# Where the last two of eight activation slots start in SBUF

## The chip, the cores and the metric

The kernel runs on one core of one Trainium2 chip. Times are device microseconds of that core; lower is better. Three runs of the kernel before took 2431.09, 2432.85 and 2435.11 us (median 2432.85).

## The reference, cut to what matters

Two transformer layers are run on 128 context tokens and 128 latent tokens, both with 2048 channels, in float32. Layer 0 mixes with differential attention beside a Conformer convolution; layer 1 mixes with an S5 state-space scan beside grouped-query attention. After each mixer there is an MLP with a squared ReLU. In short:

```
for l in range(2):
    h = rms_norm(x) * g * (1 + scale) + shift        # scale, shift, gate from ada_w[l]
    x = x + gate1 * mixer_l(h)                       # h @ w_in, heads, @ w_out
    h = rms_norm(x) * g2 * (1 + scale2) + shift2
    a = relu(h @ mlp_w1[l])                          # 2048 -> 8192
    x = x + gate2 * ((a * a) @ mlp_w2[l])            # 8192 -> 2048
y = rms_norm(x) * final
```

Every weight matrix is read once, and is multiplied by all 256 tokens.

## The kernel before

**Split products.** Activations lie channel-major: a tile is 128 channels by 256 tokens. Each float32 operand of the large products is split in two halves that TensorE takes as `float32r`: a high half (the value rounded) and a low half (value less high half). ScalarE rounds (`wh` for weights, the first 256 columns of an `hl` tile for activations) and VectorE subtracts (`wl`, and the columns 256 to 511 of `hl`). A 128x128 block of weights then takes three matmuls of 256 columns (`block`, line 517): `wh` by the high half, `wh` by the low half, `wl` by the high half. TensorE loads the 128x128 weights anew ahead of each of the three.

**Parts.** A weight piece is 128 x 1024: eight blocks, one for each of eight activation tiles. `part` (line 524) takes one piece and issues its 24 matmuls; the tiles of an operand are numbered k, and the place of a tile in its part is k % 8. A product with 2048 input channels is two parts, one on the tiles 0 to 7 and one on the tiles 8 to 15. A new piece is loaded by SP's DMA queue, rounded and subtracted while earlier parts run.

**Where the activation tiles lie.** `Arena` (line 75) is one SBUF tile, `hl`, of 12,592 float32 per partition. It holds three groups, each for the eight tiles of one half of an operand (`h0`, `h1`, `mix0`, `mix1`, `yhl`, `hid`), 4,224 elements apart (`GROUP`). Slot j of a group starts at `j * 512` elements, that is every 2,048 bytes; 128 elements of a group stay free behind its eighth slot. The arena starts at byte 42,368 of the partition, 384 past a multiple of 512; a group is 33 times 512 bytes and a half of a slot is 1,024 bytes, so the high and the low half of every slot of every group start at 384 past a multiple of 512. The weights `wh` and `wl` lie 64 past a multiple of 512, at every block.

Two kinds of tile differ. Some MLP tiles lie in the pool `hid` instead of the arena (of each MLP chunk of layer 0, and of layer 1, the tiles 0 to 7, and in one chunk of layer 1 all sixteen); these too start at 384 past a multiple of 512. And at three places the next product starts before its norm is known (`unnormed_tile`, line 816): there the tiles have 2 x 258 columns (`WIDE`), slot j starts at `j * 516` elements, so that the high halves of successive slots start at 384, 400, 416, ... 496 past a multiple of 512, and the low halves 1,032 bytes further on, at 392, 408, ... 504.

**The order of the work.** The program runs twice at build time: once to write down an order of all steps from estimated costs and due times (`charge`, `pick`), and once to issue the instructions in that order. `Arena.tile` (line 104) tells the planner when the columns that a new tile takes come free: the latest use of any tile that owned one of them. Costs do not depend on addresses.

Of the kernel before, what the change touches and what calls it, by code (L numbers as in the profile page):

```python
# [10 lines left out]
F32R = mybir.dt.float32r  # L11
# [37 lines left out]
class Engine:  # L49


    def __init__(self, kern, name, eng):
        self.kern, self.name, self.eng = kern, name, eng
# [11 lines left out]
class Pool:  # L65
# [3 lines left out]
    def tile(self, shape, dtype, name, tag=None, bufs=None):  # L69
        kw = {"tag": tag} if tag else {}  # L70
        if bufs:
            kw["bufs"] = bufs
        t = self.pool.tile(shape, dtype, name=name, **kw)
        self.kern.placed(t, (self.name, tag or name), bufs or self.bufs)
        return t


class Arena:
# [1 line left out]

    SLOT, GROUP, WIDE = 512, 8 * 512 + 128, 516

    def __init__(self, kern, pool):
        self.kern, self.n = kern, 0
        size = 2 * self.GROUP + 8 * self.WIDE
        self.all = pool.tile([128, size + 16], F32R, name="hl")
        self.name = self.all.tensor.name
        self.owner, self.mine = [None] * size, {}  # L90
        self.unused, self.groups = [0, 1, 2], {}
# [11 lines left out]

    def tile(self, part, j, wide=False):
        width = self.WIDE if wide else self.SLOT
        a = self.groups[part] * self.GROUP + j * width
        token = f"hl.{self.n}"
        self.n += 1
        k = self.kern
        k.free_at[token] = max(k.last.get(o, (0, 0))[0] for o in self.owner[a:a + width])  # L110
        self.owner[a:a + width] = [token] * width
        t = self.all[:, a:a + width]
        self.mine[id(t)] = t, token
        return t
# [1875 lines left out]
```

## Time and profile before

| | |
|---|---|
| median of 3 runs | 2432.85 us |
| profiled execution, its own time | 2435.42 us |
| span from first to last instruction | 2433.7 us |
| TensorE busy | 2349.4 us, 97% |
| VectorE, ScalarE, GpSimd busy | 70%, 47%, 7% |
| DMA | 627.64 MB, 258 GB/s |
| mean granted TensorE clock | 0.983 |

Read the row of TensorE first, then how many matmuls stand on `hl` operands, and then how far apart their starts are. The busy time of a matmul in the profile (about 280 ns) is longer than the step from one start to the next (about 118 ns), since matmuls are pipelined; the steps between starts set the time of a stream of matmuls.

### The profile page before, as it was taken

The page shows a single profiled execution, that of the slowest core. Times are in us where ns is not written, and L with a number is a line of the kernel's source. Part 1 is how long each engine was busy: PE and PEld are TensorE (multiplying, and loading weights), DVE is VectorE, ACT ScalarE, POOL GpSimd, SP SyncE. Part 2 cuts the span into 40 slices and gives each one's busy share as a digit, 9 for nine tenths or more (in the row PEclk, how much of TensorE's full clock was granted, in tenths as well). Part 3 has the DMA queues.
Part 4 walks back from the last instruction along what each step waited for, and adds up shares of the span by engine and source line. Part 5 has one row for each costly group of instructions (what it writes and reads, how often), then busy time and mean ns, then how long its engine had stood idle before and what let it go on. Part 6 is the DMA issues. An engine that isn't in the chain of part 4 may idle for free.

```text
span 2433.7 us, 49506 instructions
## 1 busy us (share of the span) xinstructions
PE 2349.4 (97%) x20152; PEld 2147.6 (88%) x20152; DVE 1698.4 (70%) x2957; ACT 1152.6 (47%) x1894; POOL 173.0 (7%) x293
## 2 busy tenths in 40 slices
PE   6999999999999999999999978999999999999997
PEld 1788887888999999999999857699999999999997
DVE  1489985677888889987666434567998855555565
ACT  2364467565434434434455644455744333443443
POOL 0000000000111011101000345000000000000000
PEclk9999999999999999999999988999999999999999
DMA  9979987879678898879877877765587755555552
GB/s 383 332 252 330 317 311 256 294 268 319 202 265 301 295 318 297 317 263 323 285 225 245 292 286 261 268 217 180 196 291 265 271 185 185 187 189 185 186 184 90
DMA packets 179637, 627.64 MB, mean 258 GB/s; under 512 B 21376, under 2 KB 21392, under 8 KB 179152
## 3 DMA queue, kind: packets, MB, share of 16 engines
q1 hardware_dynamic: 169920, 595.67, 70.6%
q0 software_dynamic: 9488, 28.81, 3.8%
q8 instruction: 158, 2.59, 0.4%
q14 instruction: 71, 0.58, 0.1%
HBM read 602.17 MB, written 26.41 MB: 258 GB/s over the span
## 4 chain that ended last, share of the span: by engine, by line
PE 86%; DMA 4%; DVE 3%; POOL 3%; ACT 3%; issue 1%; DVEq 0%; SPq 0%; ACTq 0%; POOLq 0%
PE lin L60 76%; PE ada L60 5%; POOL rt L60 2%; DMA raw<-in_ada_w 1%; DVE wl L60 1%; POOL hs L60 1%; ACT wh L60 1%; DMA raw<-in_ew_in 1%; PE m1T L60 1%; ACT hs L60 1%; PE po L60 1%; DMA raw<-m3d 1%; PE sc L60 0%; PE ps L60 0%; DMA raw<-in_w 0%
## 5 line engine op out<-in xcount | busy, mean ns | idle before, releaser
L60 PE MATMUL lin<-hl,wh 128*128 128x256 f32 (+1 forms) x11200 | 2022.1, 282 | 5.7 <-ACT wh L60 5.5
L60 PEld LDWEIGHTS lin<-hl,wh 128*128 128x128 f32 x11200 | 1718.7, 189 | 97.3 <-issue 61.5
L60 PE MATMUL lin<-hl,wl 128*128 128x256 f32 (+1 forms) x5600 | 1571.1, 281 | 11.1 <-DVE wl L60 11.0
L60 PEld LDWEIGHTS lin<-hl,wl 128*128 128x128 f32 x5600 | 1057.7, 189 | 13.7 <-DVE wl L60 13.6
L60 DVE TENSOR_TENSOR wl<-raw,wh 128x1024 fp32r<-128x1024 f32 (+1 forms) x716 | 858.6, 1207 | 283.4 <-ACT wh L60 276.3
L60 ACT CAST wh<-raw 128x1024 fp32r<-128x1024 f32 (+1 forms) x716 | 737.8, 1034 | 531.0 <-PE lin L60 285.3
L60 PE MATMUL ada<-raw,condp 128*32 128x512 f32 (+1 forms) x1408 | 190.5, 579 | 19.4 <-ACT sq L60 12.9
L60 DVE SCALAR_TENSOR_TENSOR x<-lin,mod,x 128x128 f32<-128x128 f32 x320 | 97.2, 346 | 104.5 <-PE lin L60 104.1
L60 DVE SCALAR_TENSOR_TENSOR va<-raw,condp,va 128x1024 f32<-128x1024 f32 x120 | 148.6, 1280 | 0.0
L60 ACT ACTIVATE ms<-lin 128x256 f32<-128x256 f32 x114 | 43.7, 383 | 159.4 <-PE lin L60 159.4
L60 PEld LDWEIGHTS ada<-raw,condp 128*32 128x32 f32 x1408 | 33.1, 109 | 75.6 <-DMA raw<-in_ada_w 34.8
L60 ACT CAST hl<-mq 128x256 fp32r<-128x256 f32 x128 | 51.9, 406 | 98.4 <-DVE mq L60 98.2
L60 DVE SCALAR_TENSOR_TENSOR cv<-cin,pke,cv 128x256 f32<-128x256 f32 x232 | 96.7, 478 | 0.0
L60 DVE SCALAR_TENSOR_TENSOR mq<-lin,ms 128x256 f32<-128x256 f32 x114 | 48.1, 422 | 64.9 <-ACT ms L60 64.7
L60 ACT ACTIVATE sq<-x 128x256 f32<-128x256 f32 x75 | 30.9, 416 | 116.4 <-DVE x L60 114.3
L60 DVE TENSOR_TENSOR hl<-mq,hl 128x256 fp32r<-128x256 f32 x128 | 53.8, 422 | 27.8 <-ACT hl L60 27.8
L60 POOL TENSOR_TENSOR x<-x,rb 128x512 f32<-128x512 f32 (+1 forms) x2 | 4.2, 2132 | 928.7 <-ACT rb L60 928.7
L60 DVE TENSOR_TENSOR acc<-acc,sq 128x256 f32<-128x256 f32 x75 | 31.8, 424 | 32.3 <-ACT sq L60 30.5
L60 DVE TENSOR_TENSOR hl<-h,hl 128x256 fp32r<-128x256 f32 (+1 forms) x112 | 45.4, 420 | 9.2 <-ACT hl L60 8.9
L60 ACT CAST hl<-h 128x256 fp32r<-128x256 f32 (+1 forms) x112 | 42.8, 402 | 12.5 <-DVE h L60 12.1
L60 POOL DMA_DIRECT2D m3d<-m x32 | 21.5, 677 | 348.3 <-DVE m L60 347.1
L60 DVE TENSOR_TENSOR w<-s5z,bc 128x576 f32<-128x576 f32 x64 | 45.6, 753 | 0.6
(281 smaller groups left out, 1167.5 us busy)
## 6 DMA issues: line engine op xcount, KB each, us to landing
raw<-in_w SPq DMA_DIRECT2D x512, 512.0 KB, 5.1
raw<-in_ada_w SPq DMA_DIRECT2D x352, 512.0 KB, 6.0
raw<-in_ew_in SPq DMA_DIRECT2D x68, 512.0 KB, 6.1
raw<-in_ow_in SPq DMA_DIRECT2D x40, 512.0 KB, 6.6
raw<-in_ada_w SPq DMA_DIRECT2D x64, 256.0 KB, 6.2
raw<-in_ew_out SPq DMA_DIRECT2D x32, 512.0 KB, 5.8
raw<-in_ow_out SPq DMA_DIRECT2D x32, 512.0 KB, 4.7
m3d<-m POOLq DMA_DIRECT2D x32, 256.0 KB, 6.4
```

The costliest lines, as they stand in the source:

```text
L60: return f(out, *a, **kw)
```

## The change

`Arena.tile` adds `SHIFT[j]` elements to the start of a slot with 2 x 256 columns: nothing for j = 0 to 5, 32 elements (128 bytes) for j = 6 and 40 elements (160 bytes) for j = 7. Slot 6 then starts at 0 and slot 7 at 32 past a multiple of 512 bytes, in all three groups, high and low half alike. The wide slots and the tiles of the pool stay where they are. The arena keeps its 12,592 elements (the 16 that were added at the allocation are now counted in `size`), so no other tile moves.

```diff
-    SLOT, GROUP, WIDE = 512, 8 * 512 + 128, 516
+    SLOT, GROUP, WIDE, SHIFT = 512, 8 * 512 + 128, 516, (0, 0, 0, 0, 0, 0, 32, 40)
...
-        size = 2 * self.GROUP + 8 * self.WIDE
-        self.all = pool.tile([128, size + 16], F32R, name="hl")
+        size = 2 * self.GROUP + 8 * self.WIDE + 16
+        self.all = pool.tile([128, size], F32R, name="hl")
...
-        a = self.groups[part] * self.GROUP + j * width
+        a = self.groups[part] * self.GROUP + j * width + (0 if wide else self.SHIFT[j])
```

## Rows read from the trace of the kernel before

**Rows 1.** The page: busy time of each engine, share of the span, instructions.
```profile
PE 2349.4 (97%) x20152; PEld 2147.6 (88%) x20152; DVE 1698.4 (70%) x2957; ACT 1152.6 (47%) x1894; POOL 173.0 (7%) x293
```

**Rows 2.** The page: shares of the chain that ended last, by engine and line.
```profile
PE 86%; DMA 4%; DVE 3%; POOL 3%; ACT 3%; issue 1%; DVEq 0%; SPq 0%; ACTq 0%; POOLq 0%
PE lin L60 76%; PE ada L60 5%; POOL rt L60 2%; DMA raw<-in_ada_w 1%; DVE wl L60 1%; POOL hs L60 1%; ACT wh L60 1%; DMA raw<-in_ew_in 1%; PE m1T L60 1%; ACT hs L60 1%; PE po L60 1%; DMA raw<-m3d 1%; PE sc L60 0%; PE ps L60 0%; DMA raw<-in_w 0%
```

**Rows 3.** Tile hl: operation, count, ns min/median/max, first and last start.
```profile
L60 PE MATMUL lin<-hl,wh x11200: 276/279/775, 66.4 to 2417.1; 128*128 128x256 f32 x186, 128*128 128x258 f32 x11
L60 PE MATMUL lin<-hl,wl x5600: 276/280/582, 67.7 to 2417.2; 128*128 128x256 f32 x183, 128*128 128x258 f32 x11
L60 ACT CAST hl<-h x112: 388/403/412, 58.8 to 1739.7; 128x256 fp32r<-128x256 f32 x64, 128x258 fp32r<-128x258 f32 x48
L60 DVE TENSOR_TENSOR hl<-h,hl x112: 411/419/429, 60.0 to 1741.0; 128x256 fp32r<-128x256 f32 x64, 128x258 fp32r<-128x258 f32 x48
L60 PE MATMUL ps<-hl,wh x64: 276/276/276, 1589.4 to 1608.2; 128*128 128x256 f32 x64
L60 PE MATMUL ps<-hl,wl x32: 276/276/276, 1589.6 to 1608.3; 128*128 128x256 f32 x32
```

**Rows 4.** Groups of TensorE by form: the wide matmuls, count, busy us, mean ns.
```profile
L60 PE MATMUL lin<-hl,wh 128*128 128x258 f32 x608 | 112.2, 286 | 0.0
L60 PE MATMUL lin<-hl,wl 128*128 128x258 f32 x304 | 85.9, 283 | 2.1 <-DVE wl L60 2.1
```

**Rows 5.** Chain in order of time, longest pieces: start us, length us, what.
```profile
463.38 40.35 PE lin L60 x342
...
691.67 17.88 PE lin L60 x156
...
981.56 12.25 PE lin L60 x108
...
1741.43 95.91 PE lin L60 x812
...
1932.04 485.49 PE lin L60 x4122
```

**Rows 6.** TensorE in order of time, 1589 to 1592.2 us: start, length, what.
```profile
1589.40 0.39 PE L60 MATMUL ps<-hl,wh 128*128 128x256 f32 x2
1589.63 0.28 PE L60 MATMUL ps<-hl,wl 128*128 128x256 f32 x1
...
1592.12 0.28 PE L60 MATMUL lin<-hl,wh 128*128 128x256 f32 x1
```

**Rows 7.** TensorE in order of time, 1707.1 to 1713 us, wide tiles.
```profile
1707.27 0.40 PE L60 MATMUL lin<-hl,wh 128*128 128x258 f32 x2
1707.51 0.28 PE L60 MATMUL lin<-hl,wl 128*128 128x258 f32 x1
...
1712.67 0.40 PE L60 MATMUL lin<-hl,wh 128*128 128x258 f32 x2
```

**Rows 8.** TensorE in order of time, 1720.5 to 1724.2 us, wide tiles.
```profile
1721.62 0.41 PE L60 MATMUL lin<-hl,wh 128*128 128x258 f32 x2
...
1723.83 0.41 PE L60 MATMUL lin<-hl,wh 128*128 128x258 f32 x2
```

**Rows 9.** TensorE in order of time, 550 to 552 us: from wide tiles to narrow.
```profile
550.77 0.39 PE L60 MATMUL lin<-hl,wh 128*128 128x256 f32 x2
551.00 0.28 PE L60 MATMUL lin<-hl,wl 128*128 128x256 f32 x1
551.12 0.40 PE L60 MATMUL lin<-hl,wh 128*128 128x256 f32 x2
551.36 0.28 PE L60 MATMUL lin<-hl,wl 128*128 128x256 f32 x1
551.47 0.40 PE L60 MATMUL lin<-hl,wh 128*128 128x256 f32 x2
551.71 0.28 PE L60 MATMUL lin<-hl,wl 128*128 128x256 f32 x1
551.83 0.40 PE L60 MATMUL lin<-hl,wh 128*128 128x256 f32 x2
```

**Rows 10.** Stretches: us, TensorE busy (count), granted clock, DMA share, GB/s.
```profile
1931.00:2415.00 484.00, 484.00 (x4109) 1.00 0.53 179
1572.00:1586.00 14.00, 14.00 (x125) 1.00 0.79 277
```

## The prediction

> **What bounds the kernel now.** I read the page's busy times first: TensorE is busy for 97% of the span and no other engine for over 70% [rows 1]. The chain of waits agrees: 86% of it is TensorE, 76% the matmuls that write `lin` [rows 2]. Next the count of matmuls on `hl` operands: 11,200 + 5,600 + 64 + 32 = 16,896 [rows 3], of which 608 + 304 = 912 are wide [rows 4]. The question is how far apart their starts lie. In the chain, the longest unbroken piece has 4,122 matmuls in 485.49 us [rows 5], 117.78 ns each, at the full granted clock [rows 10]; two others give 95.91 / 812 = 118.1 and 40.35 / 342 = 118.0 ns. I call this the slow rhythm. The same instruction on the same kind of addresses also runs in a quick rhythm: from 1589.40 to 1592.12 us stand 24 matmuls, 2.72 us, 113.33 ns each [rows 6], and the stretch from 1572 us shows 125 in 14 us [rows 10], 112 with the one or two cut at its edges counted whole; the chain pieces at 981.56 and 691.67 us (113.4 and 114.6 ns) are quick too [rows 5]. The clock is 1.00 in both, so it is no matter of the clock. A stream keeps its rhythm until something stops it.
>
> So about 16,896 x 117.78 ns = 1,990 us of the span is this stream, of which the chain counts 76% x 2433.7 = 1,850 us. A nanosecond more or less in each of its matmuls is therefore worth 0.93 of itself at the end.
>
> **What the change touches.** No instruction is added, removed or moved to another engine; the edits of `size` leave the allocation as it was. The pool of the MLP takes 8 of 16 tiles for each of four chunks in two layers and all 16 for one chunk, over 16 outputs each: (8 + 1) x 16 = 144 parts, 3,456 matmuls. The arena's narrow slots therefore have 16,896 - 912 - 3,456 = 12,528 matmuls, 522 parts, and two of eight slots 3,132 of them, six in a part.
>
> Three things could change. First, the writers: ScalarE's round and VectorE's subtraction into `hl` take 403 and 419 ns at the median and spread by only 24 and 18 ns over 112 tiles [rows 3], of which 48 are wide and lie at other addresses. I cost them at nothing; both engines have idle time (47% and 70% busy) [rows 1], and were every fourth of these 112 tiles 24 ns slower, it would be 0.7 us on engines that are hardly on the chain [rows 2]. Second, the planner: a narrow tile 6 now covers columns of the wide tiles 6 and 7 in place of 5 and 6, so a free time can change, but a group is given back only after the last of its readers, and costs don't depend on addresses. I cost it at nothing, give or take 1 us. Third, and this is the term that counts, the steps of TensorE between starts.
>
> **The step at another address.** No row shows a 256-column matmul anywhere but at 384 past a multiple of 512, so 0 and 32 must be bounded. The nearest rows are the wide ones, whose high halves lie at 384 to 496 in steps of 16 and whose low halves lie 8 past those. From 1707.27 to 1712.67 us stand 45 of them, 5.40 us, 120.0 ns each [rows 7]. Two columns more are worth 2 / 2.4 GHz = 0.83 ns (estimate from the two clock levels), which leaves 119.2, or 1.4 ns over the slow rhythm. The dear end is the stretch from 1721.62 to 1723.83, 18 in 2.21 us, 122.8 ns [rows 8], 122.0 without the two columns: 4.2 ns over. The cheap end is the quick rhythm, 4.45 ns under. For the 3,132 matmuls that is between -13.9 and +13.2 us. I take +1.4 ns, as the row with the most different addresses shows it: 3,132 x 1.4 = +4.4 us, times 0.93 = +4.1.
>
> **The way back.** After slot 7 a part returns to 384. Where wide tiles give way to narrow ones the first three triples last 0.35, 0.35 and 0.36 us, 1.06 together [rows 9]; three slow triples are 9 x 117.78 = 1,060 ns. So the return costs nothing that the row can show, and it ends in the slow rhythm. Between -5 and +13 ns (one triple at the cheap or the dear end) 522 returns are -2.6 to +6.8 us; I take 0.
>
> **The quick runs.** Six matmuls in every part now lie elsewhere, so a quick run in the arena cannot simply last. The two chain pieces at 691.67 and 981.56 us have 264 matmuls [rows 5], the stretch at 1572 another 125 [rows 10] and the `ps` ones 96 [rows 3]: 485 x 4.45 ns = 2.2 us that are at stake. Half of these are read from the pool or would be quick after the next stop anyway; I take +1.0, times 0.93 = +0.9.
>
> Sum: +4.1 + 0 + 0.9 = +5.0 us. The profiled execution took 2435.42 us (1.7 outside its span), 2.6 more than the median of the runs, so it would take 2440.4, and the median 2437.9; rounded, 2437.5 us.
>
> **A rule weighed.** The rows show that the same form of matmul steps at 113.3, 117.8 and about 120 ns at one clock, and that the third comes with other addresses [rows 5 to 7]. The Trainium skill, "TensorE: Matmul & The Clock Gate", section "Step-by-step: what each phase is for", says that TensorE has two independent read ports into SBUF, so that loading the next weights takes no bandwidth from the matmul that runs. By that rule addresses would not enter, and the sum would be 0. The rows speak against it in part, since the wide step is more than its two columns explain.
>
> **Rivals.** (a) The forecast: small cost, slow rhythm kept, 2437.5, own range 2430 to 2445. (b) Addresses do nothing, and what the wide rows show is the 258 columns and the odd 8 bytes of their low halves: 2432.9. For it: the writers are blind to addresses [rows 3], and slot 6 differs from the others by a whole 128 bytes. (c) The moved slots throw the stream into the quick rhythm, part by part: 18 x 522 = 9,396 matmuls at -4.45 ns are -41.8, times 0.93 -38.9, with the moved six at +4.1 that is 2398; if the 3,456 of the pool, which follow arena parts, go along (-14.3), 2384. For it: the quick rhythm exists at just these addresses and lasts once entered [rows 6, 10]. Against it: after wide tiles the stream fell back into the slow one [rows 9], and of all that runs without stop 485 us in one piece never left it [rows 5]. (d) Only the six moved matmuls are quick: -13.9 x 0.93 gives 2420. Against it: no wide stretch is on average under the slow rhythm [rows 7, 8]. (e) The other side: the moved slots step as in the dear stretch and the first triple after the return too. 13.2 + 522 x 3 x 4.2 ns = 13.2 + 6.6 = 19.8, times 0.93 = 18.4, so 2451. It decides from about 2 ns a matmul over the slow rhythm on. For it: the dear steps stand in the trace [rows 8]; against it: they came right after a stop, the settled stretch is cheaper [rows 7].
>
> **How the numbers follow.** Chances: (a) 0.35, (b) 0.12, (c) 0.22, (d) 0.10, (e) 0.21. A difference under 0.2% (4.9 us) can't be told from none: "same" is 2428 to 2437.7. (a) is cut nearly in the middle by that bound: 0.18 same, 0.17 slower. Of (e) a fifth stays inside. Faster is (c) + (d) = 0.32; same 0.18 + 0.12 = 0.30; slower the rest, 0.38. The range of 8 in 10 goes from 2390, the middle of (c), to 2452, past most of (e): half of (c), 0.11, and a third of (e), 0.07, are left out.
>
> **What would show it.** In the profile after, the long chain piece from about 1932 us holds the answer: its 4,122 matmuls in 485.49 us would become about 487 us by (a), 485.5 by (b), 472 by (c), 482 by (d) and 491 by (e). In order of time, the steps of slots 0 to 5 should stay at 353 ns a triple and the two moved triples take 357 or so. I am wrong if triples of 340 ns stand in the six unmoved slots, if the moved ones take 366 or more, or if the writers' medians move by over 20 ns.

## The result and the profile after

The changed kernel takes 2397.73 us at the median of four runs (2397.12 to 2399.99), against 2433.98 us for four runs of the kernel before (2431.09 to 2436.13): ratio 0.9852, 95% interval [0.9839, 0.9864]. It is 36 us faster, where 4.7 us slower was forecast. The time is inside the range, and it is the time of rival (c), 2398; the direction is the opposite of the forecast's. Here and below, medians and ratios leave out three single runs at a lower granted clock (0.84 in e1, 0.405 in e5, 0.936 in e11).

The instructions of every engine stand in the same order as before. So nothing but addresses has changed, and whatever moved must show in durations and steps. The first view is the page's busy time of each engine, answering to [rows 1]:

```profile
PE 2307.9 (96%) x20152; PEld 2107.8 (88%) x20152; DVE 1695.7 (71%) x2957; ACT 1153.0 (48%) x1894; POOL 173.1 (7%) x293
```

TensorE is busy 41.5 us less for the same 20,152 instructions; VectorE, ScalarE and GpSimd are within 3 us of before. The second view is tile `hl`, matmuls and writers, answering to [rows 3]:

```profile
L60 PE MATMUL lin<-hl,wh x11200: 275/276/775, 66.6 to 2379.4; 128*128 128x256 f32 x186, 128*128 128x258 f32 x11
...
L60 PE MATMUL lin<-hl,wl x5600: 276/276/582, 67.9 to 2379.6; 128*128 128x256 f32 x183, 128*128 128x258 f32 x11
...
L60 ACT CAST hl<-h x112: 388/402/412, 59.0 to 1721.7; 128x256 fp32r<-128x256 f32 x64, 128x258 fp32r<-128x258 f32 x48
L60 DVE TENSOR_TENSOR hl<-h,hl x112: 410/419/430, 60.2 to 1723.0; 128x256 fp32r<-128x256 f32 x64, 128x258 fp32r<-128x258 f32 x48
```

The writers have the medians that they had (403 and 419 ns before, 402 and 419 after): to within a nanosecond they are blind to the two new places, as forecast. The matmuls' own median length goes from 279 and 280 to 276 ns; what sets the time is the step between starts, so the third view is the chain of waits in order of time, its longest pieces (start, length, what), answering to [rows 5]:

```profile
459.77 39.39 PE lin L60 x342
...
1723.48 93.55 PE lin L60 x812
1819.17 87.84 PE lin L60 x768
1909.13 470.71 PE lin L60 x4122
```

The piece of 4,122 matmuls is the one that was singled out: 485.49 us before, 470.71 now, 114.2 ns a matmul in place of 117.78. The piece of 812 has 115.2 ns, it was 118.1. The prediction gave 487 us for (a), 485.5 for (b), 472 for (c), 482 for (d) and 491 for (e), so this row speaks for (c). The 472 takes three quarters of the whole piece for unmoved arena slots. By the addresses in the program, 1,836 of its matmuls read those, 612 read slots 6 and 7, and the rest, some 1,673, read the pool. Counted so, with the prediction's -4.45 and +1.4 ns, (c) gives 478.2 us if the arena alone turns quick and 470.7 if the pool goes along: the row shows the second. The clock is full in both, as the stretch below (columns as in [rows 10]) shows: no matter of the clock.

```profile
1909.00:2379.00 470.00, 470.00 (x4119) 470.00 (x4118) 272.24 (x358) 211.92 (x263) 0.00 (x0) 1.00 0.55 183
```

Where the saving sits within a part is seen in the fourth view, TensorE in order of time, one arena part and the first triple of the next (start, length, what; a `wh` row of two matmuls opens each triple of a slot):

```profile
1740.49 0.39 PE L60 MATMUL lin<-hl,wh 128*128 128x256 f32 x2
1740.72 0.28 PE L60 MATMUL lin<-hl,wl 128*128 128x256 f32 x1
1740.84 0.39 PE L60 MATMUL lin<-hl,wh 128*128 128x256 f32 x2
...
1741.18 0.39 PE L60 MATMUL lin<-hl,wh 128*128 128x256 f32 x2
...
1741.52 0.39 PE L60 MATMUL lin<-hl,wh 128*128 128x256 f32 x2
...
1741.86 0.39 PE L60 MATMUL lin<-hl,wh 128*128 128x256 f32 x2
...
1742.20 0.39 PE L60 MATMUL lin<-hl,wh 128*128 128x256 f32 x2
...
1742.54 0.40 PE L60 MATMUL lin<-hl,wh 128*128 128x256 f32 x2
...
1742.89 0.40 PE L60 MATMUL lin<-hl,wh 128*128 128x256 f32 x2
...
1743.25 0.39 PE L60 MATMUL lin<-hl,wh 128*128 128x256 f32 x2
```

From 1740.49 to 1742.54 stand the six slots that did not move: 2.05 us for 18 matmuls, 113.9 ns each, triples of 0.34 us but for the first (0.35). Slots 6 and 7, which moved, take 0.35 and 0.36 us, and at 1743.25 the next part begins. Over the 216 arena parts that follow another arena part without a stop, the starts in the trace give 343.0 ns for the triple of slot 0, 340.2 for each of slots 1 to 5, 353.3 for slot 6 and 356.6 for slot 7. Before, every triple of these parts was 352.4 on average. The slots that stayed where they were gained, the slots that moved did not. When this begins can be seen as well: from a stop until a stream has first passed slot 7, slots 0 to 5 step at 117.6 ns on average (2,627 steps), from then on at 113.5 ns (6,152 steps).

All `hl` steps of 256 columns, without stops and at full clock, give the account:

| matmuls | before, mean step | after | difference |
|---|---|---|---|
| arena, slots 0 to 5 (some 9,100) | 117.48 ns | 114.71 ns | -25.2 us |
| arena, slots 6 and 7 (some 2,900) | 117.47 ns | 118.01 ns | +1.6 us |
| pool `hid` (3,417) | 117.55 ns | 113.76 ns | -12.9 us |

The sum is -36.5 us; the spans differ by 2433.7 - 2396.0 = 37.7 us.

### The profile page after: what moved, and what is told of

It is laid out like the page before. It is cut to its first block, busy times and chain, and to the rows that moved or that the text cites. A ratio compares the mean times of both kernels' runs of the same rounds, so it can differ in the third digit from the quotient of the medians.

```text
span 2396.0 us, 49506 instructions
## 1 busy us (share of the span) xinstructions
PE 2307.9 (96%) x20152; PEld 2107.8 (88%) x20152; DVE 1695.7 (71%) x2957; ACT 1153.0 (48%) x1894; POOL 173.1 (7%) x293
## 4 chain that ended last, share of the span: by engine, by line
PE 85%; DMA 4%; DVE 4%; ACT 3%; POOL 3%; issue 1%; DVEq 0%; SPq 0%; ACTq 0%; POOLq 0%
PE lin L60 75%; PE ada L60 5%; POOL rt L60 2%; DMA raw<-in_ada_w 1%; DVE wl L60 1%; ACT wh L60 1%; DMA raw<-in_ew_in 1%; POOL hs L60 1%; DMA raw<-m3d 1%; PE m1T L60 1%; PE po L60 1%; ACT hs L60 0%; PE ps L60 0%; DVE hl L60 0%; DMA raw<-in_w 0%
## 5 line engine op out<-in xcount | busy, mean ns | idle before, releaser
L60 PE MATMUL lin<-hl,wh 128*128 128x256 f32 (+1 forms) x11200 | 1981.8, 281 | 5.5 <-ACT wh L60 5.0
```

Of the source, the lines that this page charges most:

```text
L60: return f(out, *a, **kw)
```

## The experiments

Every place is counted in bytes modulo 512. In the kernel before the activations are at 384 and the weights at 64, so the activations lie 384 - 64 = 320 past the weights; I call this the distance. Moved to 0 or 32, a slot has distance 448 or 480. SHIFT is in elements of four bytes. "Narrow" are the tiles of 2 x 256 columns. The diffs are against the changed kernel. The median of the kernel before on the same chip was 2433.4 to 2433.6 us for each group of runs. The letters of the theories are those of the quoted texts. The row of the trace by which I read most runs is the chain piece of 4,122 matmuls: 485.49 us is slow throughout, 467.2 (113.3 x 4,122) quick throughout.

### Which of the two moved slots does it

**Slot 7 alone at 32 (e1).**

```diff
-SHIFT = (0, 0, 0, 0, 0, 0, 32, 40)
+SHIFT = (0, 0, 0, 0, 0, 0, 0, 40)
```

> Only slot 7 is moved, by 160 bytes (32 past a multiple of 512); slot 6 stays at 384. Theory R (the return from slot 7 at 32 to slot 0 at 384 puts the stream into the quick rhythm of 113.3 ns a matmul; the moved slots themselves only cost): slots 0 to 6 step at 340 ns a triple, slot 7 at about 357, and the time is 522 x 13 ns x 0.93 = 6 us under the changed kernel, 2391 us. Theory S (it takes the two steps, 384 to 0 and 0 to 32, to get out of the slow rhythm): the slow rhythm stays, about 2433 us.

2435.93 us, ratio 1.001 [1.000, 1.002]. The long piece of the chain:

```profile
1931.20 485.83 PE lin L60 x4122
```

The gain is gone. Slot 0 now has the dear triple, 354.9 ns on average (3 x 118.3), the others about 353. A single slot at 32 does not bring the stream into the quick rhythm.

**Both at 0 (e2).**

```diff
+SHIFT = (0, 0, 0, 0, 0, 0, 32, 32)
```

> Slots 6 and 7 both 128 bytes further on, at 0 past a multiple of 512. Theory R with the place of slot 7 inside 128 bytes as what counts: 0 is the same place as 384, the stream sees nothing new, slow rhythm, 2433 us and 353 ns a triple everywhere. Theory K (any slot at another address and back kicks the stream out of the slow rhythm): quick in slots 0 to 5, 2393 to 2400 us.

2432.35 us, 0.9998 [0.9988, 1.0008]; the long piece is 485.49 us again. The moved slots step at 116.6 ns, a little under the slow rhythm, and slots 0 to 5 are back at 117.5.

**Both at 32 (e5).**

```diff
+SHIFT = (0, 0, 0, 0, 0, 0, 40, 40)
```

> Slots 6 and 7 both at 32 past a multiple of 512 (160 bytes further on). Theory L (what counts is how long the stream stays off 384 before it returns, six matmuls in place of three): quick in slots 0 to 5 as in the changed kernel, 2395 to 2402 us. Theory P (what counts is the path: the step from 0 to 32 with its own phase, and then the return): the run with slot 7 alone at 32 came back slow, so this one does too, 2433 to 2440 us.

2435.15 us, 1.0006 [0.9996, 1.0015]. Slow. So neither 0 twice nor 32 twice helps; of the layouts so far only 0 and then 32 does.

**Slot 6 at 0, slot 7 at 64 (e10), and slot 6 at 448, slot 7 at 32 (e11).**

```diff
+SHIFT = (0, 0, 0, 0, 0, 0, 32, 48)    # e10
+SHIFT = (0, 0, 0, 0, 0, 0, 16, 40)    # e11
```

> As the changed kernel (slot 6 at 0), but slot 7 at 64 past a multiple of 512 in place of 32, which is no distance at all from the weights (64). Theory H (slot 7 must start in the middle of 64 bytes for the return to come out quick): slow, 2433 us or a little over it. Theory W (two changes of place and a return are enough): quick in slots 0 to 5, 2393 to 2402 us.

2431.66 us, 0.9993 [0.9983, 1.0002].

> As the changed kernel (slot 7 at 32), but slot 6 at 448 in place of 0. Theory Z (slot 6 has to be at 0, whose distance to the weights favours the quick rhythm): slow, 2433 us. Theory W (any stop on the way to 32 will do): quick in slots 0 to 5, about 2397 us.

2396.89 us, 0.9841 [0.9823, 0.9859]. The long pieces, e10 first, then e11:

```profile
1931.67 484.14 PE lin L60 x4122
```

```profile
1910.90 469.58 PE lin L60 x4122
```

With 64 in place of 32 the stream comes back slow, with 448 in place of 0 it comes back quick. In these six layouts, what is common to the two quick ones (the change and e11) is that slot 7 is at 32 and slot 6 at neither 384 nor 32.

### What if all slots lie at one of the new places

**All arena slots at 32 (e3), all at 0 (e4).** The pool tiles stay at 384.

```diff
+SHIFT = (40, 40, 40, 40, 40, 40, 40, 40)    # e3
+SHIFT = (32, 32, 32, 32, 32, 32, 32, 32)    # e4
```

> All eight narrow slots of the arena 160 bytes further on, at 32 past a multiple of 512; the pool tiles stay at 384. Theory R: in stretches on the arena alone there is no return, so they hold one step, that of slot 7 (about 357 ns a triple, 119 a matmul); where arena and pool parts alternate, the pool part right after an arena part is quick (340). About 2433 to 2440 us in all. Theory A (32 is simply a better address): the arena-only stretches are quick, 2380 us.

2443.15 us, 1.0035 [1.0024, 1.0046]: arena steps of 118.3 ns on average, triples of 354 to 357.

> All eight narrow slots of the arena 128 bytes further on, at 0 past a multiple of 512; the pool tiles stay at 384. If only the place inside 128 bytes counts, nothing changes: 353 ns a triple, 2433 us. If the distance to the weights (64 past a multiple of 512) counts, the step of the arena-only stretches differs from 353 ns, up to the 340 of the quick rhythm (2375 us) or over it.

2411.61 us, 0.991 [0.9895, 0.9925]. Here the two rhythms of before are both seen, but the odds are turned: of the 134 streams that begin in the arena after a stop, 93 are quick, where before 10 were. The pool parts that follow, at 384, were slow in all 98 cases. Its long pieces:

```profile
1720.58 92.48 PE lin L60 x812
1815.19 90.45 PE lin L60 x768
1907.75 485.49 PE lin L60 x4122
```

**Pool tiles at 0 as well (e6).** A pad of 32 elements ahead of `hid` moves these.

```diff
+SHIFT = (32, 32, 32, 32, 32, 32, 32, 32)
+            self.pool("hpad", 1, stack=st).pool.tile([128, 32], F32, name="hpad")
```

> All narrow slots at 0 past a multiple of 512 and the MLP's pool tiles moved there too, so that no narrow part changes place. Theory D (each place of the activations against the weights has its own chance that a stream comes out of a stop in the quick rhythm; at 0 it was 93 of 134 stretches, at 384 10 of 134): about 70% of the narrow matmuls run at 113.3 ns, 15,984 x 0.65 x 4.45 x 0.93 = -43 us, about 2390 us. Theory C (it is the change of place between pool and arena that set the rhythm in the run with the arena alone at 0): without such changes nearly all is slow, 2430 us.

2399.52 us (2389.91 to 2409.61), 0.9857 [0.9817, 0.9896]. All narrow tiles lie at one place, as before, and a stream again keeps the rhythm in which it began:

```profile
1717.07 95.83 PE lin L60 x812
1815.01 87.07 PE lin L60 x768
1904.21 485.49 PE lin L60 x4122
```

118.0, 113.4 and 117.8 ns: slow, quick, slow. 102 of 146 streams after a stop are quick. That the luck of each start decides for the whole stream behind it would explain the spread of 20 us between runs: they fall in two pairs, near 2391 and near 2408.5, and the long piece alone is worth 485.5 - 467.2 = 18 us. Only one of the runs has a trace (2407.49 us, long piece slow), so this is argued and not shown.

### Place, or distance to the weights

**Activations at 384 as before, weights moved from 64 to 448 (e7): the distance of e6 at the place of before.** The pad tile and the 16 spare elements go, which moves what lies behind them.

```diff
+SHIFT = (16, 16, 16, 16, 16, 16, 16, 16)
-        size = 2 * self.GROUP + 8 * self.WIDE + 16
+        size = 2 * self.GROUP + 8 * self.WIDE
-        self.const.tile([128, 16], F32, name="pad")
+            self.pool("hpad", 1, stack=st).pool.tile([128, 32], F32, name="hpad")
```

> The narrow activations stay at 384 past a multiple of 512, pool tiles too, and the weights move from 64 to 448, so that the distance between the two is that of the run with all at 0. Theory D, with the distance as what counts: as that run, about 70% quick, 2390 us. Theory A (the activations' own place counts, whatever the weights' place): as the kernel before, 7% quick, 2433 us. The wide tiles start at 320 here; that is a few us at most.

**2383.28 us (2380.09 to 2386.39), 0.9785 [0.9769, 0.9801]: the fastest of all, 14 us under the changed kernel.** 130 of 153 streams after a stop are quick, 13,027 of their 14,899 matmuls. The long pieces are one slow, two quick:

```profile
1713.64 95.82 PE lin L60 x812
1811.58 87.08 PE lin L60 x768
1900.79 467.19 PE lin L60 x4122
```

**Activations and weights both at 0 (e8): the place of e6, distance 0.**

```diff
+SHIFT = (32, 32, 32, 32, 32, 32, 32, 32)
+        size = 2 * self.GROUP + 8 * self.WIDE
+            self.pool("hpad", 1, stack=st).pool.tile([128, 48], F32, name="hpad")
```

> Narrow activations and weights both at 0 past a multiple of 512: a third distance (0). Theory D says only that the share of quick stretches differs from both others, so the time lies between all quick (15,984 x 4.45 x 0.93 = -66 us, 2368) and all slow (2438), or there is another step altogether, as at 32 (118.3 ns). Theory A: as the run with all at 0 and the weights at 64.

2465.49 us, 1.0128 [1.0113, 1.0143]. One rhythm everywhere, 120.0 ns:

```profile
1953.17 494.63 PE lin L60 x4122
```

The same place of the activations gives 113.3 ns in most streams or 120.0 in all, by where the weights are (e6, e8); activations at 384 give mostly slow or mostly quick streams in the same way (before, e7).

**Weights at 0 and at 128, activations at 384 (e9, e12): distances 384 and 256.**

```diff
+SHIFT = (0, 0, 0, 0, 0, 0, 0, 0)
+        size = 2 * self.GROUP + 8 * self.WIDE         # e9; e12: + 32
+            self.pool("hpad", 1, stack=st).pool.tile([128, 16], F32, name="hpad")    # e12: 112
```

> Narrow activations all at 384 past a multiple of 512, weights moved from 64 to 0: a distance of 384, between that of the kernel before (320, 7% of the streams quick) and that of the runs with 448 (70 and 85%). If the share grows with the distance up to 448, it lies between: 2385 to 2430 us. If each distance has a step of its own, as 0 had (120.0 ns, one rhythm), another step can appear, 109 to 120 ns, 2305 to 2465 us. If only 448 helps, 2433.

2449.1 us, 1.006 [1.0045, 1.0075]: 118.7 ns, one rhythm.

> Narrow activations all at 384, weights at 128 past a multiple of 512: a distance of 256. Theory D: another share of quick streams, or another step; 2305 to 2465 us. If the distances 0 and 256 are alike (half the 512 bytes apart), 120.0 ns and about 2465 us; if 256 goes on from 320 downward, all slow, 2436 us.

2466.96 us, 1.0135 [1.0119, 1.0152]: 120.0 ns, one rhythm. e9's and e12's long pieces:

```profile
1943.59 489.16 PE lin L60 x4122
```

```profile
1948.13 494.64 PE lin L60 x4122
```

**Every narrow tile at 416, weights at 448 (f4): the distance of e3, 480, at another place.**

```diff
+SHIFT = (24, 24, 24, 24, 24, 24, 24, 24)     # on e7, with a pad of 40
```

> Every narrow tile, arena and pool, at 416 past a multiple of 512 with the weights at 448: distance 480, which e3 had at another place (32 past, weights at 64) with triples of 354 to 357. Theory 'distance': steps of 118.3 ns and about 2443 us, as e3. Rival 'place' (it is where the operands lie, not how far apart): no reason for e3's figures; a quick stream would give about 2383 us, one rhythm of 120 ns 2466.

2447.46 us, 1.0051 [1.0035, 1.0068], mean arena step 118.4 ns where e3 had 118.3. The long piece, 118.3 ns:

```profile
1941.45 487.79 PE lin L60 x4122
```

Together:

| distance, mod 512 | kernels | step of settled streams |
|---|---|---|
| 0 | e8 | 120.0 ns |
| 256 | e12 | 120.0 ns |
| 320 | before | 117.8, seldom 113.3 |
| 384 | e9 | 118.7 ns |
| 448 | e6, e7 | 113.3 in most streams, else 117.8 |
| 480 | e3, f4 | 118.3 ns |

Two distances (448, 480) were tried at two places each, with the same rhythms both times; two places (0, 384) at several distances, with different ones. It is the distance that selects the rhythms. Three things stay open. The odds do not seem to be set by the distance alone: at 448, 102 of 146 streams are quick in the one trace of e6 and 130 of 153 in that of e7, and the slowest run of e7 (2386.39 us) is under the fastest of e6 (2389.91). The period of 512 bytes is not shown: 0 and 256 give the same 120.0 ns, so a period of 256 would fit the table as well. And the edits that move the weights move the other tiles behind the arena too; these are not the cause, at least, of the differences between e7 and f4 or between e8 and e9, where the weights and those tiles lie at the same places and only the activations differ.

### Does an odd slot help or hurt a stream that is quick by its distance

**On e7, slot 7 at distance 480 (f1), slots 6 and 7 at 480 and 0 (f2), slot 7 at 0 (f3).**

```diff
+SHIFT = (16, 16, 16, 16, 16, 16, 16, 24)    # f1
+SHIFT = (16, 16, 16, 16, 16, 16, 24, 32)    # f2
+SHIFT = (16, 16, 16, 16, 16, 16, 16, 32)    # f3
```

> As e7 (every narrow tile at distance 448 from the weights, modulo 512; 2383.3 us, most streams quick), but slot 7 of each arena part lies 32 bytes further on, at distance 480. Theory P (the last step of the way round decides in which rhythm the stream comes back, and a way back from 480 alone comes back slow, as in e1): the 18 or so matmuls a part that were quick go to 117.8 ns, about 2383 + 0.85 x 16,000 x 4.45 ns x 0.93 = 2439 us, triples of 353 in slots 0 to 6. Theory D (only the distance of each slot counts, and distance 448 is quick whatever stood before it): slot 7 costs 1,566 x (118.3 - 113.3) x 0.93 = 7 us more, 2391 us, triples of 340 in slots 0 to 6. Under 2380: the odd slot helps the streams that were slow in e7.

2429.14 us, 0.9983 [0.9973, 0.9993].

> As e7, with slot 6 at distance 480 and slot 7 at distance 0 (32 and 64 bytes further on). Theory P: the way back leaves from distance 0, after which e10 and all the parts of e2 came back slow at distance 320: about 2439 us. Theory D: slots 6 and 7 cost 1,566 x 5.0 and 1,566 x 6.7 ns, times 0.93 17 us, so 2400 us, with triples of 340 in slots 0 to 5.

2396.79 us, 0.9848 [0.9833, 0.9863].

> As e7, with slot 7 alone at distance 0 (64 bytes further on). Theory P: returns slow, about 2439 us. Theory D: 1,566 x (120.0 - 113.3) x 0.93 = 10 us more, 2393 us, triples of 340 in slots 0 to 6. If f1 comes back slow and f3 quick, it is the 480 that makes it slow; the other way round, the 0.

2390.12 us, 0.9822 [0.9808, 0.9837]. The long pieces of f1, f2 and f3:

```profile
1924.64 485.69 PE lin L60 x4122
```

```profile
1909.76 471.95 PE lin L60 x4122
```

```profile
1902.82 469.24 PE lin L60 x4122
```

One slot in eight, 32 bytes further on, undoes 46 of e7's 50 us (f1: slots 1 to 6 step at 116.8 ns on average, where e7 has 114.2); the same slot 64 bytes further on costs 7 us (f3: slots 1 to 6 at 114.0). In f1 the turn comes where it came in the changed kernel, the other way: slots 0 to 5 step at 114.8 ns until a stream has first passed slot 7, and at 117.7 afterwards. Theory P was right for f1 and wrong for f2 and f3, theory D the other way round. So it is neither the distance alone nor any disturbance: from 480 a stream comes back slow to 448, from 0 quick (in f2 after a first triple of 352 ns on average). All ways round that were run, as distances:

| slots 0 to 5, slot 6, slot 7 | kernel | the stream comes back |
|---|---|---|
| 320, 320, 480 | e1 | slow |
| 320, 480, 480 | e5 | slow |
| 320, 448, 448 | e2 | slow |
| 320, 448, 0 | e10 | slow |
| 320, 448, 480 | the change | quick |
| 320, 384, 480 | e11 | quick |
| 448, 448, 480 | f1 | slow |
| 448, 448, 0 | f3 | quick |
| 448, 480, 0 | f2 | quick |

The rhythm in which a stream comes back depends on where it has been, and not on the last slot alone (e1 and the change both come from 480). I know of no simple rule that fits all nine rows, and what TensorE or SBUF does there was not seen: that stays open. An obvious thought, that the read of the next weights and the read of the moving columns meet, fits the role of the distance and is only argued.

## Why the prediction was wrong

- *What bounds the kernel.* Right. TensorE's steps set the time: the mean step of all narrow matmuls went from 117.49 to 115.12 ns, times 15,984 is 37.9 us, and the span fell by 37.7. The weight of 0.93 was a little low here.
- *The writers and the planner at nothing.* Right: medians within 1 ns, the same order of instructions.
- *The step at another address.* Forecast 119.2 ns a moved matmul; measured 118.01 on average, triples of 353.3 and 356.6 where "357 or so" was said. Against the mean before it is +1.6 us, +4.1 was forecast. The sign is right and the size 2.6 times too large (0.54 ns over the mean before, where 1.4 was taken); the wide rows that it came from stand at other distances, and e2 shows moved slots under the slow rhythm (116.6).
- *The way back.* **This is the step that failed**, with "it ends in the slow rhythm". The return costs 343.0 - 340.2 = 3 ns in the first triple, as good as the nothing that was said, but it ends in the quick rhythm: 9,100 unmoved matmuls at -2.77 ns and, since the stream carries its rhythm into the pool, 3,417 there at -3.79: -25.2 and -12.9 us. The row that I leaned on [rows 9] shows one return from wide tiles. Their last slots stand at other distances than 448 and 480, and by e1, e2, e5 and e10 most ways round come back slow: the row was true and spoke of another way round. The lower bound of -5 ns a return was also not what it was called: one triple at the cheap end is 3 x -4.45 = -13 ns.
- *The quick runs.* The reason was wrong. "A quick run in the arena cannot simply last" when six matmuls lie elsewhere: it need not last, since each part makes it anew.
- *The rivals.* (c) named the mechanism and gave 2398. Its size agrees partly by chance: -38.9 us were put on the arena's unmoved slots (measured -25.2, since after a stop a stream stays slow until it has passed slots 6 and 7 once, 117.6 ns against 113.5 afterwards: the mean of 114.71 ns lies 31% of the way from the quick rhythm to the slow) and the pool was left out, which brought -12.9 of the -14.3 that its variant allowed. The variant with the pool, 2384, is what happened in settled streams and is 14 us too low for the whole, mostly for the same reason. (c) got a chance of 0.22. Against it stood the 485 us that never left the slow rhythm; but that piece never changed its place, so it said nothing of what changing places does. The chances hold a slip: the fifth of (e) that "stays inside" was not added to "same", which by the prediction's own terms is 0.34, and slower 0.34.
- *The rule weighed.* The steps move with the distance, from 113.3 to 120.0 ns at one clock and one form of instruction (e7, e8). The Trainium skill, "TensorE: Matmul & The Clock Gate", section "Step-by-step: what each phase is for", has two independent read ports, so that loading the next weights takes no read bandwidth from the running matmul. The prediction read this as "addresses would not enter". By that reading e7, e9 and e12, with the activations at 384 and the weights at 448, 0 and 128, would have taken one time; they took 2383.28, 2449.1 and 2466.96 us, so the measurement decides against the reading for this stream. Whether the read ports have a part in it, no run shows.

## What to carry to other kernels

Where a long stream of like matmuls has two rhythms in one trace at one clock, look for something cheap that selects between them: here it was the place of the operands. Rows from undisturbed stretches cannot price an edit that disturbs the stream at every part: give the rival in which the rhythm flips its full weight. Measure the step between starts, not the matmul's length, and look at where weights and activations lie against each other modulo 512 bytes: here a few spare elements are worth from -50 to +33 us out of 2433. Aim at the good distance for all tiles (e7) rather than at a lucky way round (the change), which one slot can undo (e1, f1).

## What the runs showed of the hardware

- The same 128x128 by 256-column `float32r` matmul, streamed without a stop at a granted clock of 1.00, steps at 113.3, 117.8, 118.3, 118.7 or 120.0 ns, by the distance between its activations and its weights, counted here modulo 512 bytes (table above). The best and the worst, e7 and e12, differ by 84 us in time.
- At distances 320 and 448 two rhythms, 113.3 and 117.8 ns, exist side by side. The one in which a stream of constant distance settles in its first few matmuls after a stop lasts until the next stop, over 4,122 matmuls in one piece (before, e6, e7).
- A single odd slot in eight can set the rhythm of the other seven (f1: 2429.14 us where e7 has 2383.28), and one at another distance does not (f3: 2390.12 us).
